# Latents stored before their norms' factors, norm sums read from transposed sums, and one mask product instead of two

## The chip, the cores and the metric

The kernel runs on one core of a Trainium2 chip. The metric is the device time of one execution in microseconds (us): the median over three runs of the kernel before is 1730.43 us (1730.31 to 1732.46). "The kernel before" is the program without the change; the profile below was taken of one of its executions.

A core has five engines that work through their own instruction streams in order and meet at semaphores: PE multiplies matrices, ACT applies functions and copies, DVE does elementwise work and reductions, POOL does small work and issues some DMAs, SP issues the other DMAs. PE writes to PSUM, which has eight banks of 128 x 512 float32 each; ACT and DVE carry results from there to SBUF.

## The reference

The program is a trunk of two layers over 512 tokens of width 1024, in float32. Each layer adds two blocks to the token stream `x`:

```
x = x + OutProj(sum over i of sigmoid(gate_i) * BranchProj_i(mixer_i(RMSNorm(x))))
x = x + ConvFFN(RMSNorm(x))
```

The three mixers are neighbourhood attention on a grid (NA), latent attention (MLA, four heads), and windowed grouped attention with sinks (GQA, eight heads). They share one input projection. What matters here:

```
def rmsnorm(x, g):   y = x * rsqrt(mean(x*x) + EPS);  return y * g
MLA: q  = rmsnorm(c_q,  g_qa)  @ w_uq      c_q: 384 wide,  a projection of rmsnorm(x)
     kv = rmsnorm(c_kv, g_kva) @ w_ukv     c_kv: 256 wide, a projection of rmsnorm(x)
     p  = softmax((q_nope k_nope + rope(q_pe) rope(k_pe)) * 192 ** -0.5);  out = p v
GQA: scores with |i - j| > 128 are masked; a sink logit joins the softmax
```

Since an RMS norm multiplies each token by one number, that number can be applied to the input or to whatever is linear in it. There are two norms in a row in front of MLA: the norm of `x` (one factor per token, called r1 below), and the norm of the latent `c_q` or `c_kv`.

## The kernel before, in words

Activations lie with features on the partitions and the 512 tokens along the free dimension. Each product in float32 is made of three products of rounded parts: `mm3` (L158) issues, for each block of 128 rows, high by high (L162), low weights or activations by high (L163) and high by low (L164), each with 512 columns. `split` (L145) makes the two parts: ACT casts the high one (L148, or L151 with a factor), DVE subtracts it (L149, L152). Weights come by DMA into `raw` (three buffers), are split into `whi` and `wlo` (three buffers each), and are fetched three entries ahead of their use. So a weight's cast waits until PE is through with the weight three entries earlier.

The order of PE's and SP's work is written out by hand in `schedule` (a list of steps, run one by one); the orders of ACT and DVE are set by a scheduler at build time, which sees priorities (`PRIO`, `ATTN_PRIO`) and its own estimates. On the chip every engine keeps the order that it was given.

The factor of a norm is made in three steps. `sumsq` adds the squares of the feature blocks (ACT squares, DVE adds), `rs_tokens` (L184) adds over the partitions with four products of `acc` by a column of ones (L188), takes the mean on DVE (L190) and the power -1/2 on POOL (L192), which leaves a tile `rt` of 128 x 4 (a factor per token, tokens on partitions). `rs_spread` (L195) turns it with four transpositions (L200) into `rb`, the factor along the free dimension, repeated on all partitions.

The front of the MLA stage runs so in each layer: the products `lat` (four latent blocks) and `lat4` (the fifth), with the norm sums and the spread of r1 in between; `latent` multiplies each block by `rb` (L155), squares it, and, for the key and value blocks, splits it. Then `rs_q` (sums of the query latent), `kr` (the rotary key, L424), `rb_q` (spread of the query factor, which multiplies the three query blocks again on DVE before they are split), `rs_k`, the values `v`, a gate, `rb_k`, then the rotary queries `qr`, the first head's `qn` and `kn`, a gate, the second head's, and the attention.

The attention steps: `ms(h, half)` makes the scores of two blocks of 128 queries (L492 to L496, five products each, in one of three banks `ps_s`), then DVE takes the negated row maximum (`nm`, L498), ACT the exponential with its row sum (`pt`, L500), DVE the reciprocal (L501) and ACT the scaling (L502). `mt(h, half)` transposes `pt` of all four blocks (L509) and splits the result into `ph`, `pl`; `mp(h, half)` multiplies by the values into `ps_po`, which `split` moves to `yah`, `yal`. PE's order there is `ms(h+1, 0)`, `mt(h, 0)`, `qn` and `kn` of head h+2, `mp(h, 0)`, `mt(h, 1)`, `ms(h+1, 1)`, `mp(h, 1)`, and then the same for the next h.

In GQA, `gs` makes the scores of one head and one query block (L761, L762), adds the masks of the left and right neighbour blocks by products with an identity in bf16 (L764, L766; both in the two inner blocks of queries, one in each outer block), and goes on as MLA does, with two score banks.

## Time and profile before

| | value |
|---|---|
| time, median of 3 runs | 1730.43 us (1730.31 to 1732.46) |
| the profiled execution | 1730.6 us |
| its span in the trace | 1728.8 us |
| PE busy | 1715.1 us, 99% |
| DVE busy | 1155.6 us, 67% |
| ACT busy | 857.9 us, 50% |
| POOL busy | 31.2 us, 2% |
| share of PE in the chain that ended last | 91% |

The span is the time from the first to the last traced instruction; 1.8 us of the execution lie around it. Matmuls overlap: the next one starts long before the end that the trace draws for the last, so the distance between two starts is what a product costs PE, not its drawn length. A time in square brackets behind an instruction is how long its engine sat idle before it, and what it waited for.

### The profile page before, as it was taken

The page shows a single profiled execution, that of the slowest core. Times are in us where ns is not written, and L with a number is a line of the kernel's source. Part 1 is how long each engine was busy: PE and PEld are TensorE (multiplying, and loading weights), DVE is VectorE, ACT ScalarE, POOL GpSimd, SP SyncE. Part 2 cuts the span into 40 slices and gives each one's busy share as a digit, 9 for nine tenths or more (in the row PEclk, how much of TensorE's full clock was granted, in tenths as well). Part 3 has the DMA queues.
Part 4 walks back from the last instruction along what each step waited for, and adds up shares of the span by engine and source line. Part 5 has one row for each costly group of instructions (what it writes and reads, how often), then busy time and mean ns, then how long its engine had stood idle before and what let it go on. Part 6 is the DMA issues. An engine that isn't in the chain of part 4 may idle for free.

```text
span 1728.8 us, 21460 instructions
## 1 busy us (share of the span) xinstructions
PE 1715.1 (99%) x8106; PEld 1427.5 (83%) x8106; DVE 1155.6 (67%) x1872; ACT 857.9 (50%) x1492; POOL 31.2 (2%) x74
## 2 busy tenths in 40 slices
PE   9999999999999999999999999999999999999998
PEld 7788888888888888888887888888788888888887
DVE  6767885877558777734357678768875587777234
ACT  6774655665335444433247656557544354444232
POOL 1000000000000000000000000000000000000000
PEclk9999999999999999999999999999999999999999
DMA  5222233222333333323232232332223333333231
GB/s 175 72 77 83 80 95 94 68 68 62 105 91 116 96 95 97 97 89 107 80 92 83 74 86 71 99 90 68 62 73 110 97 98 98 98 98 98 85 104 67
DMA packets 290695, 155.38 MB, mean 90 GB/s; under 512 B 8672, under 2 KB 287072, under 8 KB 290592
## 3 DMA queue, kind: packets, MB, share of 16 engines
q1 hardware_dynamic: 288288, 148.92, 29.9%
q0 software_dynamic: 2016, 4.72, 0.9%
q8 instruction: 63, 1.03, 0.2%
q10 hardware_dynamic: 288, 0.38, 0.1%
q14 instruction: 40, 0.33, 0.1%
HBM read 151.89 MB, written 2.10 MB: 89 GB/s over the span
## 4 chain that ended last, share of the span: by engine, by line
PE 91%; DVE 4%; ACT 2%; issue 2%; DMA 0%; SPq 0%; POOLq 0%; POOL 0%; DVEq 0%; ACTq 0%
PE ps_d L162 20%; PE ps_d L164 20%; PE ps_d L163 20%; PE ps_g L163 7%; PE ps_g L162 7%; PE ps_g L164 7%; DVE wlo L149 1%; PE ps_po L653 1%; PE ps_tp L789 1%; PE ps_tp L638 1%; PE ps_tp L509 1%; ACT rsw L211 1%; PE ps_s L761 0%; PE ps_s L620 0%; PE ps_s L619 0%
## 5 line engine op out<-in xcount | busy, mean ns | idle before, releaser
L148 ACT CAST whi<-raw 128x1024 fp32r<-128x1024 f32 (+4 forms) x340 | 302.2, 889 | 611.9 <-PE ps_d L163 330.6
L162 PE MATMUL ps_d<-hh,whi 128*128 128x512 f32 x1328 | 520.5, 392 | 0.0
L164 PE MATMUL ps_d<-hh,wlo 128*128 128x512 f32 x1328 | 517.1, 389 | 0.0
L163 PE MATMUL ps_d<-hl,whi 128*128 128x512 f32 x1328 | 516.9, 389 | 0.0
L149 DVE TENSOR_TENSOR wlo<-raw,whi 128x1024 fp32r<-128x1024 f32 (+3 forms) x338 | 345.1, 1021 | 199.6 <-ACT whi L148 199.1
L164 PEld LDWEIGHTS ps_d<-hh,wlo 128*128 128x128 f32 x1328 | 249.3, 188 | 52.3
L162 PEld LDWEIGHTS ps_d<-hh,whi 128*128 128x128 f32 x1328 | 249.5, 188 | 50.6 <-DVE rot L155 0.6
L163 PEld LDWEIGHTS ps_d<-hl,whi 128*128 128x128 f32 x1328 | 249.5, 188 | 50.3
L162 PE MATMUL ps_g<-ff,whi 128*128 128x512 f32 x334 | 129.9, 389 | 0.0
L163 PE MATMUL ps_g<-ff,whi 128*128 128x512 f32 x334 | 129.9, 389 | 0.0
L164 PE MATMUL ps_g<-ff,wlo 128*128 128x512 f32 x334 | 129.9, 389 | 0.0
L155 DVE TENSOR_TENSOR u<-ps_d,rb 128x512 f32<-128x512 f32 x80 | 55.3, 691 | 65.0 <-PE ps_d L164 65.0
L155 DVE TENSOR_TENSOR gz<-ps_d,rb 128x512 f32<-128x512 f32 x48 | 33.2, 691 | 76.5 <-PE ps_d L164 76.3
L851 ACT ACTIVATE c<-u,par 128x512 f32<-128x512 f32 x88 | 71.7, 815 | 5.1 <-DVE u L155 2.8
L149 DVE TENSOR_TENSOR pl<-ps_tp,ph 128x512 fp32r<-128x512 f32 x104 | 69.2, 682 | 6.7 <-ACT ph L148 6.6
L162 PEld LDWEIGHTS ps_g<-ff,whi 128*128 128x128 f32 x334 | 62.7, 188 | 13.1
L164 PEld LDWEIGHTS ps_g<-ff,wlo 128*128 128x128 f32 x334 | 62.7, 188 | 13.0
L163 PEld LDWEIGHTS ps_g<-ff,whi 128*128 128x128 f32 x334 | 62.7, 188 | 12.9
L853 DVE SCALAR_TENSOR_TENSOR c<-u,par,c 128x511 f32<-128x511 f32 x88 | 66.0, 750 | 2.7
L852 DVE SCALAR_TENSOR_TENSOR c<-u,par,c 128x511 f32<-128x511 f32 x88 | 65.6, 745 | 0.6 <-ACT c L851 0.6
L857 ACT ACTIVATE c<-c 128x512 f32<-128x512 f32 x44 | 27.8, 631 | 76.6 <-DVE c L853 76.6
L148 ACT CAST ph<-ps_tp 128x512 fp32r<-128x512 f32 x104 | 57.6, 587 | 5.9 <-PE ps_tp L509 2.8
(280 smaller groups left out, 2624.6 us busy)
## 6 DMA issues: line engine op xcount, KB each, us to landing
raw<-in_w_in_dram SPq DMA_DIRECT2D x86, 512.0 KB, 3.9
raw<-in_w_up_dram SPq DMA_DIRECT2D x80, 512.0 KB, 3.7
raw<-in_w_down_dram SPq DMA_DIRECT2D x32, 512.0 KB, 3.5
raw<-in_w_down_dram SPq DMA_DIRECT2D x16, 384.0 KB, 3.0
raw<-in_w_in_dram SPq DMA_DIRECT2D x18, 256.0 KB, 2.9
raw<-in_w_br_mla_dram SPq DMA_DIRECT2D x16, 256.0 KB, 2.6
raw<-in_w_br_na_dram SPq DMA_DIRECT2D x16, 256.0 KB, 2.6
raw<-in_w_br_gqa_dram SPq DMA_DIRECT2D x16, 256.0 KB, 2.6
```

The source lines that it names most:

```text
L148: nc.scalar.copy(hi, src)
L149: nc.vector.tensor_sub(lo, src, r32(hi))
L155: self.nc.vector.tensor_tensor(out, a, b, ALU.mult)
L162: mm(ps, sh, mh, start=first and k == 0, stop=False)
L163: mm(ps, sh, ml, start=False, stop=False)
L164: mm(ps, sl, mh, start=False, stop=last and k == n - 1)
L211: nc.scalar.copy(sw[32 * i:32 * i + 32, :], ps[32 * j:32 * j + 32, :])
L509: self.nc.tensor.transpose(tp[:, b * P:(b + 1) * P], self.pts[h, b][:, kc * P:(kc + 1) * P], self.idf)
L851: nc.scalar.activation(c, u, AF.Identity, bias=pr[:, PC_CB + fi:PC_CB + fi + 1], scale=cw[:, 1:2])
L852: nc.vector.scalar_tensor_tensor(c[:, 1:], u[:, :S - 1], cw[:, 0:1], c[:, 1:], ALU.mult, ALU.add)
L853: nc.vector.scalar_tensor_tensor(c[:, :S - 1], u[:, 1:], cw[:, 2:3], c[:, :S - 1], ALU.mult, ALU.add)
L857: nc.scalar.activation(c, c, AF.Gelu_apprx_tanh)
```

## The change

Four things change.

1. `latent` no longer multiplies by `rb`. The blocks are split straight from PSUM, and squared straight from PSUM. The query blocks are not multiplied by their own factor either: `rb_q` is gone with its four transpositions. The missing factors are applied later: the query's (times r1 and the softmax scale) as the scale operand of the exponential, and by one more small DVE instruction on the maximum, `nm`; the key's and value's in the split of the values and in `rb_k`, which carried the latent norm's factor already.
2. `rs_tokens` transposes the four blocks of `acc` and lets DVE add along the free dimension; the mean and epsilon move from DVE to POOL. For the two latent norms POOL also multiplies the sums by r1 squared, and the result by r1 (or by r1 times the softmax scale). POOL runs two, or four, instructions where it ran one.
3. The step `qr` moves from behind `rb_k` to between `rs_k` and the values.
4. In the two inner query blocks of GQA one mask product over both neighbour blocks takes the place of two.

The diff (empty lines left out):

```diff
--- before.py
+++ after.py
@@ -181,27 +181,32 @@
         nc.vector.tensor_add(acc, acc, sq)
         return acc
-    def rs_tokens(self, pool, acc, dim):
+    def rs_tokens(self, acc, dim, latent=None):
         nc = self.nc
         ps = self.bank("r")
         for j in range(4):
-            nc.tensor.matmul(ps[:, j:j + 1], acc[:, j * P:(j + 1) * P], self.ones, start=True, stop=True)
+            nc.tensor.transpose(ps[:, j * P:(j + 1) * P], acc[:, j * P:(j + 1) * P], self.idf)
         ms = self.small.tile([P, 4], F32, tag="ms", name="ms", bufs=2)
-        nc.vector.tensor_scalar(ms, ps[:, 0:4], 1.0 / dim, EPS, ALU.mult, ALU.add)
+        nc.vector.tensor_reduce(ms, ps[:].rearrange("p (j c) -> p j c", j=4), AX.X, ALU.add)
+        if latent:
+            nc.gpsimd.tensor_tensor(ms, ms, latent[0], ALU.mult)
+        nc.gpsimd.tensor_scalar(ms, ms, 1.0 / dim, EPS, ALU.mult, ALU.add)
         rt = self.small.tile([P, 4], F32, tag="rt", name="rt", bufs=3)
         nc.gpsimd.tensor_tensor(rt, ms, self.neghalf, ALU.pow)
+        if latent:
+            nc.gpsimd.tensor_tensor(rt, rt, latent[1], ALU.mult)
         return rt
-    def rs_spread(self, rt, rb, scale=None):
+    def rs_spread(self, rt, rb):
         ps = self.bank("r")
         for j in range(4):
             self.nc.tensor.transpose(ps[:, j * P:(j + 1) * P], rt[:, j:j + 1].to_broadcast([P, P]), self.idf)
-        if scale is None:
-            self.nc.scalar.copy(rb, ps)
-        else:
-            self.nc.scalar.activation(rb, ps, AF.Copy, scale=scale)
+        self.nc.scalar.copy(rb, ps)
     def rope(self, pool, ps, rows, ct, st, nb=2):
         nc = self.nc
@@ -272,7 +277,7 @@
                             for k0, nk in ((0, 8), (8, 8), (16, 6)) for m in range(4)]
         gate = iter([("gate", b, m) for b in (1, 0, 2) for m in range(8)]).__next__
-        s = ["mla_open", "lat", "lat4", "rs_q", "kr", "rb_q", "rs_k", ("v", 0), ("v", 1), gate(), "rb_k", "qr"]
+        s = ["mla_open", "lat", "lat4", "rs_q", "kr", "rs_k", "qr", ("v", 0), ("v", 1), gate(), "rb_k"]
         s += [("qn", 0), ("kn", 0), gate(), "mla_attn", ("qn", 1), ("kn", 1), ("ms", 0, 0), ("ms", 0, 1), gate()]
         for h in range(3):
             dn = [("qn", h + 2), ("kn", h + 2)] if h < 2 else [("naq", 0)]
@@ -349,19 +354,12 @@
         self.split(hi, lo, self.x[k], g[:, k:k + 1])
         self.h.append((hi, lo))
-    def norm_hooks(self, evac, late=False):
-        def sums():
-            self.rt = self.rs_tokens(self.const, self.acc, D)
-        def spread():
-            self.rb = self.const.tile([P, S], F32, tag="rb", name="rb")
-            self.rs_spread(self.rt, self.rb)
-            evac(0)
-            evac(1)
-        if late:
-            return {(1, 0): sums, (1, 2): lambda: (spread(), evac(2)), (1, 3): lambda: evac(3)}
-        return {(0, 3): sums, (1, 1): spread, (1, 2): lambda: evac(2), (1, 3): lambda: evac(3)}
+    def norm_sums(self):
+        self.rt = self.rs_tokens(self.acc, D)
+    def norm_spread(self):
+        self.rb = self.const.tile([P, S], F32, tag="rb", name="rb")
+        self.rs_spread(self.rt, self.rb)
     def do_mla_open(self):
@@ -389,10 +387,17 @@
         return self.mxt(f"{t}h{k}", F32R), self.mxt(f"{t}l{k}", F32R)
     def do_lat(self):
-        self.c, self.lat, self.qacc, self.kacc = [], [None] * 5, None, None
+        self.lat, self.qacc, self.kacc = [None] * 5, None, None
         self.qtags, self.ktags = ["acc", "sq1"], ["yah0", "yal0"]
-        self.group(self.W["lat"], self.h, 
-                   self.norm_hooks(lambda i: self.latent(LAT[i], self.gbank[i]), self.l == 0))
+        lat = lambda j: self.latent(LAT[j], self.gbank[j])
+        early = [(0, 3), (1, 1)] if self.l else [(1, 0), (1, 2)]
+        hooks = {(1, j): [lambda j=j: lat(j)] for j in range(4)}
+        hooks.setdefault(early[0], []).append(self.norm_sums)
+        hooks.setdefault(early[1], []).append(self.norm_spread)
+        self.group(self.W["lat"], self.h, {k: (lambda fs=fs: [f() for f in fs]) for k, fs in hooks.items()})
+        self.r1 = self.small.tile([P, 8], F32, tag="r1", name="r1")
+        self.nc.gpsimd.tensor_tensor(self.r1[:, 0:4], self.rt, self.rt, ALU.mult)
+        self.nc.gpsimd.tensor_scalar(self.r1[:, 4:8], self.rt, MLA_SCALE, None, ALU.mult)
     def do_lat4(self):
         if self.l == 0:
@@ -401,20 +406,18 @@
         self.latent(4, self.dense(self.spec(), self.h))
     def latent(self, i, ps):
+        tags = ((f"mg{i}", f"mg{i + 4}") if i < 3 else ("mg3", "mg7") if i == 3 else ("yah3", "yal3"))
+        self.lat[i] = [self.mxt(t, F32R) for t in tags]
+        self.split(*self.lat[i], ps, self.pr[:, PC_QA + i:PC_QA + i + 1])
         if i < 3:
-            c = self.mxt(("yah1", "yal1", "yah2")[i])
-            self.mul(c, ps, self.rb)
-            self.qacc = self.sumsq(self.const, c, self.qacc, self.qtags)
-            self.c.append(c)
-            return
-        c = self.mp.tile([P, S], F32, tag="ev", name="ev", bufs=2)
-        self.mul(c, ps, self.rb)
-        self.kacc = self.sumsq(self.mx, c, self.kacc, self.ktags)
-        self.lat[i] = self.mxt(("mg3", "yah3")[i - 3], F32R), self.mxt(("mg7", "yal3")[i - 3], F32R)
-        self.split(*self.lat[i], c, self.pr[:, PC_QA + i:PC_QA + i + 1])
+            self.qacc = self.sumsq(self.const, ps, self.qacc, self.qtags)
+        else:
+            self.kacc = self.sumsq(self.mx, ps, self.kacc, self.ktags)
     def do_rs_q(self):
-        self.rtq = self.rs_tokens(self.mp, self.qacc, 384.0)
+        self.rtq = self.rs_tokens(self.qacc, 384.0, [self.r1[:, 0:4], self.r1[:, 4:8]])
     def do_kr(self):
         st = self.weights(self.spec())
@@ -431,16 +434,8 @@
         self.stack(self.kr[0], t, 0)
         self.swap(self.kr[1], self.kr[0])
-    def do_rb_q(self):
-        rbq = self.mxt("yal2")
-        self.rs_spread(self.rtq, rbq, MLA_SCALE)
-        for i in range(3):
-            self.mul(self.c[i], self.c[i], rbq)
-            self.lat[i] = self.mxt(f"mg{i}", F32R), self.mxt(f"mg{i + 4}", F32R)
-            self.split(self.lat[i][0], self.lat[i][1], self.c[i], self.pr[:, PC_QA + i:PC_QA + i + 1])
     def do_rs_k(self):
-        self.rtk = self.rs_tokens(self.mp, self.kacc, 256.0)
+        self.rtk = self.rs_tokens(self.kacc, 256.0, [self.r1[:, 0:4], self.rt])
     def do_v(self, half):
         if half == 0:
@@ -496,8 +491,9 @@
             mm(s, self.qr[h][:, bs], self.kr[1], start=False, stop=True)
             nm = self.small.tile([P, 2], F32, tag="nm", name="nm", bufs=6)
             nc.vector.tensor_reduce(nm[:, 0:1], s, AX.X, ALU.max, negate=True)
+            nc.vector.tensor_scalar(nm[:, 0:1], nm[:, 0:1], self.rtq[:, b:b + 1], None, ALU.mult)
             pt = self.mp2.tile([P, S], F32, tag="pt", name="pt", bufs=6)
-            nc.scalar.activation(pt, s, AF.Exp, bias=nm[:, 0:1], accum_out=nm[:, 1:2])
+            nc.scalar.activation(pt, s, AF.Exp, bias=nm[:, 0:1], scale=self.rtq[:, b:b + 1], accum_out=nm[:, 1:2])
             nc.vector.reciprocal(nm[:, 1:2], nm[:, 1:2])
             nc.scalar.activation(pt, pt, AF.Copy, scale=nm[:, 1:2])
             self.pts[h, b] = pt
@@ -760,10 +756,9 @@
             s = self.bank("s")
             mm(s[:, :w], self.gqs[h][:, bs], self.gk[g][0][:, ks], start=True, stop=False)
             mm(s[:, :w], self.gqs[h][:, bs], self.gk[g][1][:, ks], start=False, stop=False)
-            if b > 0:
-                mm(s[:, 0:P], self.idb, self.gmask[:, 0:P], start=False, stop=b == 3)
-            if b < 3:
-                mm(s[:, w - P:w], self.idb, self.gmask[:, P:2 * P], start=False, stop=True)
+            sv = s[:, :w].rearrange("p (k c) -> p k c", c=P)[:, (nk - 1 if b == 0 else 0):(1 if b == 3 else nk):2]
+            mm(sv, self.idb, self.gmask[:].rearrange("p (k c) -> p k c", c=P)[:, b == 0:2 - (b == 3)],
+               start=False, stop=True)
             nc.vector.tensor_reduce(nm[:, hh:hh + 1], s[:, :w], AX.X, ALU.max, negate=True)
             nc.vector.tensor_scalar(nm[:, hh:hh + 1], nm[:, hh:hh + 1], HD_SCALE, self.nsink[:, h:h + 1],
                                     ALU.mult, ALU.min)
@@ -838,7 +833,9 @@
             self.fps, self.fp = self.open("ff")
             self.ff = []
             ups = [0, NF, 1, NF + 1]
-            self.group(self.W["up"], self.h, self.norm_hooks(lambda i: self.conv(ups[i], self.gbank[i])))
+            conv = lambda *js: [self.conv(ups[j], self.gbank[j]) for j in js]
+            self.group(self.W["up"], self.h, {(0, 3): self.norm_sums, (1, 1): lambda: (self.norm_spread(), conv(0, 1)),
+                                              (1, 2): lambda: conv(2), (1, 3): lambda: conv(3)})
         else:
             self.conv(fi, self.dense(self.spec(), self.h))```

The scheduler at build time makes new orders for ACT and DVE in the MLA stage of each layer, and at one place of GQA. Three places matter; both layers have the same order. Numbers in names tell buffers apart.

On ACT, at the second head of the attention. `ps_po_...` is the product `mp(0, 1)`, `pt_960`, `pt_972` (before) and `pt_957`, `pt_970` (after) are the last two query blocks of head 1, `pt_994` and `pt_993` the first of head 2. Before:

```order
L500 ACTIVATE pt_960,nm_958<-ps_s_952,nm_958 128x512
L500 ACTIVATE pt_972,nm_970<-ps_s_964,nm_970 128x512
L148 CAST yah0_982<-ps_po_927 128x512
L502 ACTIVATE pt_960<-pt_960,nm_958 128x512
L502 ACTIVATE pt_972<-pt_972,nm_970 128x512
L500 ACTIVATE pt_994,nm_992<-ps_s_986,nm_992 128x512
```

On ACT at the same place of the changed program:

```order
L148 CAST yah0_980<-ps_po_923 128x512
L496 ACTIVATE pt_957,nm_954<-ps_s_948,nm_954,rt_440 128x512
L496 ACTIVATE pt_970,nm_967<-ps_s_961,nm_967,rt_440 128x512
L498 ACTIVATE pt_957<-pt_957,nm_954 128x512
L496 ACTIVATE pt_993,nm_990<-ps_s_984,nm_990,rt_440 128x512
L498 ACTIVATE pt_970<-pt_970,nm_967 128x512
```

The cast of `ps_po` moved ahead of the two exponentials, and an exponential of the next head moved between the two scalings. The same happens one head later.

On DVE, at the same place (`yal` is the low part of `ps_po`). Before:

```order
L498 TENSOR_REDUCE nm_958<-ps_s_952 128x1
L498 TENSOR_REDUCE nm_970<-ps_s_964 128x1
L501 RECIPROCAL nm_958<-nm_958 128x1
L501 RECIPROCAL nm_970<-nm_970 128x1
L498 TENSOR_REDUCE nm_992<-ps_s_986 128x1
L149 TENSOR_TENSOR yal0_983<-ps_po_927,yah0_982 128x512
```

On DVE at the same place of the changed program:

```order
L493 TENSOR_REDUCE nm_954<-ps_s_948 128x1
L493 TENSOR_REDUCE nm_967<-ps_s_961 128x1
L494 TENSOR_SCALAR nm_954<-nm_954,rt_440 128x1
L494 TENSOR_SCALAR nm_967<-nm_967,rt_440 128x1
L149 TENSOR_TENSOR yal0_981<-ps_po_923,yah0_980 128x512
L493 TENSOR_REDUCE nm_990<-ps_s_984 128x1
L497 RECIPROCAL nm_954<-nm_954 128x1
L494 TENSOR_SCALAR nm_990<-nm_990,rt_440 128x1
L497 RECIPROCAL nm_967<-nm_967 128x1
```

The two reciprocals now stand behind the low part of `ps_po` and behind the next head's maximum.

On ACT, in the front of the MLA stage, between the values and the second gate (`whi` 128x1024 is that gate's weight). Before:

```order
L225 CAST kr<-kr 64x512
L224 CAST kr<-kr 64x512
L211 COPY rsw<-ps_d 32x512 x4
L148 CAST whi<-raw 128x1024
L211 COPY rsw<-ps_d 32x512 x4
```

On ACT in the changed program, from the copies of the rotary key (`ev`) towards that weight:

```order
L216 COPY rsw<-ev 32x512 x2
L216 COPY rsw<-ps_d 32x512 x4
L148 CAST whi<-raw 128x384
L151 ACTIVATE ynh_564<-ps_d,rt 128x512
L225 CAST kr<-rot 64x512
L216 COPY rsw<-ps_d 32x512 x4
L151 ACTIVATE ynh_575<-ps_d,rt 128x512
L151 ACTIVATE ynh_586<-ps_d,rt 128x512
L230 CAST kr<-kr 64x512
L148 CAST whi<-raw 128x256
L151 ACTIVATE ynh_597<-ps_d,rt 128x512
L225 CAST qr<-rot 64x512 x2
```

Behind the last of these rows come one more `kr` cast, two more `qr` casts, and then the gate's weight: all of the rotary queries' work on ACT now precedes it.

## Rows read from the trace of the kernel before

**Rows 1.** The page, part 1: busy us (share of span) and instructions.
```profile
PE 1715.1 (99%) x8106; PEld 1427.5 (83%) x8106; DVE 1155.6 (67%) x1872; ACT 857.9 (50%) x1492; POOL 31.2 (2%) x74
```

**Rows 2.** Waits of PE: us in total, times, longest.
```profile
PE ps_s L492 <- ACT pt L500: 2.7, 2, 1.3
...
PE ps_po L163 <- DVE pl L149: 0.5, 2, 0.2
```

**Rows 3.** Timeline of PE around norm sums and spread: start us, us, instruction.
```profile
21.00 0.94 PE L188 MATMUL ps_r<-cst,acc 128*128 128x1 f32 x8
...
22.13 0.40 PE L163 MATMUL ps_g<-hl,whi 128*128 128x512 f32 x1
...
27.16 0.39 PE L164 MATMUL ps_g<-hh,wlo 128*128 128x512 f32 x1
27.39 0.60 PE L200 MATMUL ps_r<-idf,rt 128*128 128x128 f32 x4
...
28.06 0.39 PE L163 MATMUL ps_g<-hl,whi 128*128 128x512 f32 x1
```

**Rows 4.** Timeline of PE, scores and masks of an inner GQA block.
```profile
375.26 0.34 PE L762 MATMUL ps_s<-gk,gq 128*128 128x384 f32 x1
375.44 0.23 PE L764 MATMUL ps_s<-gmask,idb 128*128 128x128 bf16 x1
...
375.54 0.42 PE L761 MATMUL ps_s<-gk,gq 128*128 128x384 f32 x1
375.79 0.34 PE L762 MATMUL ps_s<-gk,gq 128*128 128x384 f32 x1
```

**Rows 5.** Timeline, all engines, first attention scores of layer 0.
```profile
72.98 1.28 DVE L498 TENSOR_REDUCE nm<-ps_s 128x1 f32<-128x512 f32 x2
...
73.70 0.69 ACT L500 ACTIVATE pt<-ps_s,nm 128x512 f32<-128x512 f32 x1 [0.91 <-DVE nm L498]
...
74.53 0.50 PE L492 MATMUL ps_s<-kn,qn 128*128 128x512 f32 x1 [1.33 <-ACT pt L500]
```

**Rows 6.** ACT's groups by form, 40 to 70 us: busy us, mean ns.
```profile
L211 ACT COPY rsw<-ps_d 32x512 f32<-32x512 f32 x8 | 4.6, 579 | 0.1
L151 ACT ACTIVATE ynh<-ps_d,rt 128x512 fp32r<-128x512 f32 x4 | 2.7, 686 | 1.0 <-POOL rt L192 0.9
L220 ACT CAST qr<-rot 64x512 fp32r<-64x512 f32 x4 | 2.5, 620 | 1.1 <-DVE rot L215 1.0
L148 ACT CAST whi<-raw 128x1024 fp32r<-128x1024 f32 x2 | 2.1, 1053 | 0.0
```

**Rows 7.** Timelines of DVE and PE at the second gate of layer 0.
```profile
59.75 1.22 DVE L149 TENSOR_TENSOR wlo<-raw,whi 128x1024 fp32r<-128x1024 f32 x1
...
61.24 0.39 PE L164 MATMUL ps_d<-hh,wlo 128*128 128x512 f32 x1
```

**Rows 8.** Timelines of ACT, DVE, PE at `mt(1, 0)` of layer 0.
```profile
92.84 0.69 ACT L500 ACTIVATE pt<-ps_s,nm 128x512 f32<-128x512 f32 x1 [1.97 <-DVE nm L498]
...
94.18 0.58 ACT L148 CAST yah<-ps_po 128x512 fp32r<-128x512 f32 x1
94.65 1.35 ACT L502 ACTIVATE pt<-pt,nm 128x512 f32<-128x512 f32 x2
...
95.00 0.69 DVE L498 TENSOR_REDUCE nm<-ps_s 128x1 f32<-128x512 f32 x1 [0.52 <-PE ps_s L496]
...
96.81 0.15 DVE L501 RECIPROCAL nm<-nm 128x1 f32<-128x1 f32 x1
...
95.94 1.04 PE L509 MATMUL ps_tp<-idf,pt 128*128 128x128 f32 x8
```

**Rows 9.** Timelines of POOL and DVE in the front of layer 0's MLA stage.
```profile
37.24 1.93 POOL L192 TENSOR_TENSOR rt<-ms,cst 128x4 f32<-128x4 f32 x1 [13.74 <-DVE ms L190]
42.77 1.01 POOL L192 TENSOR_TENSOR rt<-ms,cst 128x4 f32<-128x4 f32 x1 [3.59 <-DVE ms L190]
...
37.08 1.23 DVE L149 TENSOR_TENSOR wlo<-raw,whi 128x1024 fp32r<-128x1024 f32 x1
```

## The prediction

> **What bounds the kernel now.** I read the busy times first: PE works for 99% of the span, DVE for 67%, ACT for half of it, POOL for next to nothing [rows 1]. So an instruction taken from PE is worth its whole price, one taken from DVE or ACT is worth something only where PE waits for it. Then I read PE's waits [rows 2]: the longest is 1.3 us, once per layer, for the first scores of MLA, and all waits together are few. What the list does not show are stalls that hide under the drawn ends of products; distances between starts show them. A 512-column product costs 0.23 us of PE (27.16 to 27.39) [rows 3] though it is drawn 0.39 long; I use 0.227, the mean of long stretches. The reader is to see that PE has almost no slack and that almost every stall is in MLA's attention or in GQA: any wait that a new order of ACT and DVE makes there goes straight into the time.
>
> **What PE loses in work.** The sum is made against the profiled execution, 1730.6 us (span 1728.8 and 1.8 around it), which is 0.2 above the median of 1730.43.
>
> Norm sums: the eight passes over the ones column and the product behind them take from 21.00 to the next product's start at 22.13, 1.13 us; less one product, 0.90 [rows 3]. Four transpositions, measured likewise at the spread, take 28.06 - 27.39 - 0.227 = 0.44. There are four norm sums per layer (two norms of `x`, two of latents), eight in all: 8 x 0.46 = 3.7 us saved. The new ones move 128 columns just as those of the spread do, so I take that price as it is.
>
> The query factor's spread goes: 2 x 0.44 = 0.9 us.
>
> Masks: 32 inner pairs (2 layers, 2 key heads, 2 inner blocks, 4 heads). From the second score product to the next scores' second product it is 375.79 - 375.26 = 0.53 us with a pair between; two 384-column products alone cost about 2 x 0.17 (0.18 to the mask) [rows 4]. So a pair costs 0.19. A single product of 256 columns saves at most the second's share, some 0.07, and at least nothing, since the same columns pass. By columns (128 more cost about 0.055, the step from 384 to 512 columns) I take 0.02: 32 x 0.02 = 0.7 us, with bounds 0 and 2.3.
>
> Work in all: 5.3 us less. The one added chain, DVE's reduction over 512 columns in place of 4 (0.69 against some 0.15) and one to three more POOL instructions, lies beside two weights' products (over 5 us) between each norm sum and its spread. That cover is large: the norms of `x` stay hidden.
>
> **What PE loses or gains in waits, per layer.** I follow ACT and DVE in their new orders, with durations from the rows, in layer 0's times; layer 1 has the same order.
>
> First scores. PE waits 1.33 us by the trace because DVE comes to the first maxima only at 72.98, with a backlog, and the bank is free only after the exponential of 73.70 [rows 5]; counted by starts the stall is 1.5. Now DVE has eight multiplications of 0.67 less in front and two longer reductions more, so the backlog is gone. From the scores' start at s: the first are ready at s + 1.3, the maximum takes 0.69, the low part of `kn`, which stands between, 0.6, the new scaling 0.1, the exponential 0.69, the release some 0.1, that is s + 3.5 to 3.7; PE wants the bank at s + 3.4. Stall 0.1 to 0.3 instead of 1.5: a gain of 1.2, with bounds 0 and 1.5.
>
> Second gate. PE asks for the low part of its weight at 61.24 and it is ready at 59.75 + 1.22 = 60.97 [rows 7]; a slack of 0.27. With three sums and a spread saved PE asks at 61.24 - 3 x 0.46 - 0.44 = 59.4. On ACT all copies and casts of the rotary queries now stand in front of this weight's cast. PE's rotary key ends 83 products and two turns earlier, at 39.8; then the first gate's cast (1.05), its low part (1.22), DVE's longer reduction (0.69) and two steps of the key (1.3) must pass before ACT may copy: 44.1. From there ACT does ten copies (0.58 to 0.62), four value parts (0.69), four query casts (0.62), three key casts of the same length and two small weights (0.9 together) [rows 6]: 13.8 drawn, about 13.4 start to start, then the cast of 1.05 and DVE's 1.22. That gives 59.9: PE waits 0.6 us. Bounds 0 (ACT a little quicker) and 2.
>
> Head 2's first transpositions, `mt(1, 0)`. Before, ACT takes the exponentials at 92.84, the cast of `ps_po` at 94.18, both scalings from 94.65 to 96.0, and PE transposes from 95.94, the last block some 0.3 later: just in time [rows 8]. In the new order ACT sits at the cast of `ps_po` until its product has ended, about 93.9. Then it runs the cast (0.5), two exponentials (0.7 each, to 95.7), and waits for the reciprocal, which DVE has behind the low part and head 2's maximum (95.0 to 95.7 even before): 95.9. Scaling (0.6), head 2's exponential (0.7), second scaling (0.7): 97.9. PE needs it at 96.3. Wait 1.6, with the restart 1.75. Bounds 0.5 and 2.2. No other work is in PE's queue: it is in order, and the transpositions hold up `qn` and `kn` of head 3, which do not need them.
>
> Behind it PE comes 1.75 later to `mp(1, 1)`, where it loses 0.9 now waiting for low parts (the list shows 0.5 of it in both layers together [rows 2], the rest is under drawn ends). DVE's queue there hangs on `kn` of head 3, so it moves along; I get 0.5, a gain of 0.4.
>
> The next head, `mt(2, 0)`: the same order, the same count from the end of `ps_po`: 1.5, bounds 0.5 and 2.2. Head 3 has a gate of 5.4 us between; no wait.
>
> GQA: at one place per layer a 1.05 us weight cast [rows 6] now stands ahead of an exponential whose bank PE waits for; two banks, about 0.3, bounds 0 and 1.
>
> Per layer: -1.2 + 0.6 + 1.75 - 0.4 + 1.5 + 0.3 = +2.55; twice: 5.1 us.
>
> **Sum.** 1730.6 - 5.3 + 5.1 = 1730.4 us. What the change takes from PE, its new order in the attention gives back.
>
> **POOL.** The latent factors now pass through four POOL instructions. One power took 1.01 us, and one 1.93, when it was issued beside a DVE subtraction with both inputs in SBUF (37.08 to 38.31) [rows 9]. The trace has no POOL multiplication of this shape; the power is the nearest row and bounds it from above, nothing from below. DVE's reduction ends at about 42.8 and ACT needs the value factor at 48.1: 5.3 us for four instructions. At 1.01 each they take 4.0: hidden. The query factor is wanted 25 us later.
>
> The Trainium skill (SBUF — State Buffer, section Who interferes with whom) says that a DVE instruction with two SBUF inputs contends with a GpSimd instruction that reads SBUF, and that the later one blocks until the other is done. The 1.93 us row agrees, since it ends about one power after the subtraction's end; by that rule each of the four can be held up by the rotary key's multiplications, which is the second rival below.
>
> **The rivals.**
>
> Faster: the two new waits before the transpositions do not come, since the cast of `ps_po` and the products meet otherwise than I count. For it: the wait rests on sums of ten steps, and both blocks were in time before. Against it: the order is fixed and each step has a row. Then only 1.2 is gained at the first scores, 0.6 lost at the gate, 0.3 in GQA: -5.3 + 2 x (-1.2 + 0.6 + 0.3) = -5.9, so 1724.7; with half of the waits, 1727.5.
>
> Slower: the value factor comes late. At 1.93 for each POOL instruction it is ready at 42.8 + 7.7 = 50.5, 2.4 us after ACT needs it, and ACT's chain to the second gate hangs on it: PE waits 0.6 + 2.4 there. That is 2 x 2.4 more, 1735.2. It decides from a chain of 5.3 us on. For it: the row of 1.93 is of this very stage. Against it: during the chain DVE has only two such instructions and then idles.
>
> Not what it says: transpositions of `acc` or the strided mask cost more than their kin, so that less than 5.3 is saved; without any of the mask and half of the sums, 1733.
>
> **How the numbers follow.** A difference under 0.2% (3.5 us) cannot be told from none for this kernel. Forecast (1727 to 1734, its own range): 0.47. Faster rival: 0.28. Slower rival: 0.17; less saved: 0.08, half of it beyond 3.5 us when waits are longer as well. So faster 0.28, same 0.47 + 0.04 = 0.51, slower 0.17 + 0.04 = 0.21. The range reaches from 1725.3, close to the faster rival, to 1734.6, short of the slower one.
>
> **What would show it.** In the profile after: the norm sums as four transpositions with the next product 0.6 us behind; PE's wait at the first scores down from 1.3 to at most 0.3; in the list of PE's waits a new entry, transpositions waiting for ACT's scaled `pt`, twice per layer, 1 to 2 us each; a wait of about half a us at the second gate for `wlo`; POOL's four instructions ended 5 us after DVE's reduction. The forecast is wrong if PE's transpositions wait under 0.5 us, or if the second gate waits over 2.

## The result, and the profile after

The changed kernel takes 1732.93 us (median of 20 runs, 1732.27 to 1735.04), the kernel before 1730.70 us in the 20 runs beside them. The ratio is 1.0014 with a 95% interval of 1.0008 to 1.0020: 2.2 us slower, small but real. The forecast was 1730.4 us, no change; the time lies above it, inside the range. The profiled execution took 1732.3 us (span 1730.5).

Part 1 of the page, in the form of [rows 1]:

```profile
PE 1711.9 (99%) x8034; PEld 1420.3 (82%) x8034; DVE 1156.5 (67%) x1888; ACT 858.2 (50%) x1490; POOL 38.4 (2%) x94
```

PE is busy 3.2 us less and the program is longer all the same: time went into waits. PE's waits in the changed kernel (us in total, times, longest), to be read against [rows 2]:

```profile
PE ps_tp L505 <- ACT pt L498: 4.0, 4, 1.0
PE ps_d L164 <- DVE wlo L149: 1.7, 2, 0.9
PE ps_s L487 <- ACT pt L496: 1.2, 4, 0.3
PE ps_tp L784 <- DVE pt L775: 1.2, 4, 0.3
...
PE ps_r L191 <- DVE acc L181: 0.7, 2, 0.4
```

All five are new, new in kind or longer. The first is the wait before `mt(1, 0)` and `mt(2, 0)` that was forecast; the second is the second gate, also forecast, but at about half its size; the fourth stands before transpositions in GQA and was 0.5 us in two places before; the fifth, transpositions that wait for the sum of the key latent's squares, was not forecast. The 2.7 us of [rows 2] at the first scores are gone: what is left there is part of the third.

The norm sum and the spread, PE's timeline (start us, us), against [rows 3]:

```profile
20.63 0.60 PE L191 MATMUL ps_r<-idf,acc 128*128 128x128 f32 x4
20.99 0.47 PE L162 MATMUL ps_g<-hh,whi 128*128 128x512 f32 x1
21.30 0.39 PE L163 MATMUL ps_g<-hl,whi 128*128 128x512 f32 x1
```

From 20.63 to the second product at 21.30 it is 0.67 us, that is 0.44 for four transpositions beside one product of 0.227, as counted.

The first scores of layer 0, timelines of DVE, ACT and PE, against [rows 5]:

```profile
70.48 0.69 DVE L493 TENSOR_REDUCE nm<-ps_s 128x1 f32<-128x512 f32 x1
...
71.93 0.78 ACT L496 ACTIVATE pt<-ps_s,nm,rt 128x512 f32<-128x512 f32 x1 [1.15 <-DVE nm L494]
...
72.85 0.50 PE L487 MATMUL ps_s<-kn,qn 128*128 128x512 f32 x1
```

The first maximum is taken at 70.48 instead of 72.98, so the bank is free in time but for 0.3 us by starts.

`mt(1, 0)` of layer 0, timelines of ACT, DVE and PE, against [rows 8]:

```profile
92.25 0.59 ACT L148 CAST yah<-ps_po 128x512 fp32r<-128x512 f32 x1 [3.03 <-PE ps_po L164]
92.73 0.78 ACT L496 ACTIVATE pt<-ps_s,nm,rt 128x512 f32<-128x512 f32 x1
...
94.26 0.72 ACT L498 ACTIVATE pt<-pt,nm 128x512 f32<-128x512 f32 x1
94.89 0.76 ACT L496 ACTIVATE pt<-ps_s,nm,rt 128x512 f32<-128x512 f32 x1
...
95.64 0.71 ACT L498 ACTIVATE pt<-pt,nm 128x512 f32<-128x512 f32 x1
...
91.67 0.33 DVE L494 TENSOR_SCALAR nm<-nm,rt 128x1 f32<-128x1 f32 x2
...
93.66 0.50 PE L487 MATMUL ps_s<-kn,qn 128*128 128x512 f32 x1 [0.32 <-ACT pt L496]
...
96.41 0.77 PE L505 MATMUL ps_tp<-idf,pt 128*128 128x128 f32 x5 [0.99 <-ACT pt L498]
```

ACT is idle for 3.03 us, the scaled maxima are there at 92.0, and the exponentials wait behind a cast whose product ends at 92.2. They come 0.7 late, so PE misses a score bank at 93.66, and the second scaling, behind an exponential of the next head, lets PE go on only at 96.41. The wait at the bank, 0.6 us by starts (see the experiments), was not forecast. It adds nothing to the sum: PE goes on when the second scaling has ended, and what it lost at the bank it waits less there.

The second gate of layer 0, timelines of ACT, DVE and PE, against [rows 7]:

```profile
57.53 1.05 ACT L148 CAST whi<-raw 128x1024 fp32r<-128x1024 f32 x1
...
57.90 1.41 DVE L226 TENSOR_TENSOR qr<-rot,qr 64x512 fp32r<-64x512 f32 x2
59.34 1.69 DVE L149 TENSOR_TENSOR wlo<-raw,whi 128x1024 fp32r<-128x1024 f32 x2
...
60.62 0.50 PE L164 MATMUL ps_d<-hh,wlo 128*128 128x512 f32 x1 [0.92 <-DVE wlo L149]
```

ACT casts the weight at 57.53, near to where my sum puts it (59.9 less 1.22 and 1.05 is about 57.6; this run is 0.3 ahead from its first 16 us, so the sum was right to 0.3). But DVE then has two subtractions of the rotary queries in front, and the low part starts 0.76 after the cast has ended.

The front of the MLA stage in layer 0, ACT, DVE and PE at the key latent's sum:

```profile
36.11 0.68 ACT L151 ACTIVATE yah<-ps_d,par 128x512 fp32r<-128x512 f32 x1
38.34 0.60 ACT L180 ACTIVATE sq<-ps_d 128x512 f32<-128x512 f32 x1 [1.55 <-DVE yal L152]
...
35.82 0.69 DVE L193 TENSOR_REDUCE ms<-ps_r 128x4 f32<-128x512 f32 x1 [3.12 <-PE ps_r L191]
36.43 1.21 DVE L149 TENSOR_TENSOR wlo<-raw,whi 128x1024 fp32r<-128x1024 f32 x1
37.56 0.74 DVE L152 SCALAR_TENSOR_TENSOR yal<-ps_d,par,yah 128x512 fp32r<-128x512 f32 x1
38.97 0.69 DVE L181 TENSOR_TENSOR acc<-acc,sq 128x512 f32<-128x512 f32 x1 [0.66 <-ACT sq L180]
...
39.05 0.39 PE L427 MATMUL ps_d<-hl,whi 128*128 128x512 f32 x1
39.72 0.66 PE L191 MATMUL ps_r<-idf,acc 128*128 128x128 f32 x4 [0.28 <-DVE acc L181]
```

ACT's square reads the same bank `ps_d` as DVE's low part `yal`, and stands behind it: here the readers of one bank on two engines follow one another. Of ACT's 1.55 us of waiting, 0.74 are this low part; before it DVE was busy with the low part of a weight, from 36.43 to 37.64. So the sum is made at 39.66, PE wanted it at 39.28. This agrees with the Trainium skill (PSUM — Partial Sum Buffer, section PSUM bank collisions raise a hardware error): two engines may not access one bank and quadrant at once, reads included, so software orders them.

### The profile page after: what moved, and what is told of

The parts are those of the page before. It is cut to its first block, busy times and chain, and to the rows that moved or that the text cites. A ratio compares the mean times of both kernels' runs of the same rounds, so it can differ in the third digit from the quotient of the medians.

```text
span 1730.5 us, 21339 instructions
## 1 busy us (share of the span) xinstructions
PE 1711.9 (99%) x8034; PEld 1420.3 (82%) x8034; DVE 1156.5 (67%) x1888; ACT 858.2 (50%) x1490; POOL 38.4 (2%) x94
## 3 DMA queue, kind: packets, MB, share of 16 engines
q8 instruction: 63, 1.03, 0.3%
## 4 chain that ended last, share of the span: by engine, by line
PE 93%; ACT 3%; DVE 3%; issue 1%; POOLq 0%; POOL 0%; DVEq 0%; ACTq 0%
PE ps_d L162 21%; PE ps_d L164 21%; PE ps_d L163 21%; PE ps_g L163 7%; PE ps_g L164 7%; PE ps_g L162 7%; PE ps_tp L784 1%; PE ps_po L649 1%; PE ps_tp L634 1%; ACT pt L496 1%; PE ps_s L757 1%; PE ps_tp L505 1%; DVE wlo L149 1%; PE ps_s L758 0%; ACT rsw L216 0%
## 5 line engine op out<-in xcount | busy, mean ns | idle before, releaser
L148 ACT CAST whi<-raw 128x1024 fp32r<-128x1024 f32 (+4 forms) x340 | 302.2, 889 | 606.7 <-PE ps_d L163 339.5
L162 PE MATMUL ps_d<-hh,whi 128*128 128x512 f32 x1328 | 520.5, 392 | 0.0
L164 PE MATMUL ps_d<-hh,wlo 128*128 128x512 f32 x1328 | 517.3, 390 | 1.7 <-DVE wlo L149 1.7
L163 PE MATMUL ps_d<-hl,whi 128*128 128x512 f32 x1328 | 517.0, 389 | 0.0
L149 DVE TENSOR_TENSOR wlo<-raw,whi 128x1024 fp32r<-128x1024 f32 (+3 forms) x338 | 344.9, 1021 | 189.9 <-ACT whi L148 189.5
L164 PEld LDWEIGHTS ps_d<-hh,wlo 128*128 128x128 f32 x1328 | 249.3, 188 | 54.7 <-DVE wlo L149 2.6
L162 PEld LDWEIGHTS ps_d<-hh,whi 128*128 128x128 f32 x1328 | 249.6, 188 | 50.8 <-DVE rot L155 0.5
L163 PEld LDWEIGHTS ps_d<-hl,whi 128*128 128x128 f32 x1328 | 249.5, 188 | 50.2
L162 PE MATMUL ps_g<-ff,whi 128*128 128x512 f32 x334 | 129.9, 389 | 0.0
L163 PE MATMUL ps_g<-ff,whi 128*128 128x512 f32 x334 | 129.9, 389 | 0.0
L164 PE MATMUL ps_g<-ff,wlo 128*128 128x512 f32 x334 | 129.9, 389 | 0.0
L155 DVE TENSOR_TENSOR u<-ps_d,rb 128x512 f32<-128x512 f32 x80 | 55.3, 691 | 65.1 <-PE ps_d L164 65.1
L155 DVE TENSOR_TENSOR gz<-ps_d,rb 128x512 f32<-128x512 f32 x48 | 33.2, 691 | 78.3 <-PE ps_d L164 78.0
L162 PEld LDWEIGHTS ps_g<-ff,whi 128*128 128x128 f32 x334 | 62.7, 188 | 13.1
L164 PEld LDWEIGHTS ps_g<-ff,wlo 128*128 128x128 f32 x334 | 62.7, 188 | 13.0
L163 PEld LDWEIGHTS ps_g<-ff,whi 128*128 128x128 f32 x334 | 62.7, 188 | 13.0
L149 DVE TENSOR_TENSOR pl<-ps_tp,ph 128x512 fp32r<-128x512 f32 x104 | 68.6, 682 | 6.0 <-ACT ph L148 5.9
L148 ACT CAST ph<-ps_tp 128x512 fp32r<-128x512 f32 x104 | 57.0, 585 | 7.3 <-PE ps_tp L505 3.9
```

The costliest lines, as they stand in the source:

```text
L148: nc.scalar.copy(hi, src)
L149: nc.vector.tensor_sub(lo, src, r32(hi))
L155: self.nc.vector.tensor_tensor(out, a, b, ALU.mult)
L162: mm(ps, sh, mh, start=first and k == 0, stop=False)
L163: mm(ps, sh, ml, start=False, stop=False)
L164: mm(ps, sl, mh, start=False, stop=last and k == n - 1)
```

## The experiments

Times are medians, each beside the kernel before on the same chip; intervals are 95%. They are about 0.1% (1.6 us) to either side, so smaller effects are read from two traces: the start of the same product in both, and the places where the distance of the two jumps. "By starts" means this; the first 16 us, which differ from run to run, are left out of it.

**The square ahead of the split** (the changed kernel with)

```diff
     def latent(self, i, ps):
-        self.split(*self.lat[i], ps, self.pr[:, PC_QA + i:PC_QA + i + 1])
         if i < 3:
             self.qacc = self.sumsq(self.const, ps, self.qacc, self.qtags)
         else:
             self.kacc = self.sumsq(self.mx, ps, self.kacc, self.ktags)
+        self.split(*self.lat[i], ps, self.pr[:, PC_QA + i:PC_QA + i + 1])
```

> The changed kernel with the square of each latent block ahead of its split. Theory (the second latent sum comes late because ACT's square stands behind DVE's low part of the same bank): PE's wait of its transpositions for the sum (0.7 us in two entries, 0.44 and 0.60 by starts) goes, about 1.0 us in all, 1731.9 us. Rival (the sum is late because DVE is busy with a 1.2 us weight part at that time, whatever the square does): the wait stays at 0.7 and the time at 1732.9.

1731.24 us beside 1730.29: 0.9 above before instead of 2.2 (ratio 1.0006, 0.9997 to 1.0015). By starts 0.44 and 0.60 less, at these two transpositions and nowhere else. In its trace, ACT, DVE and PE:

```profile
36.15 0.59 ACT L180 ACTIVATE sq<-ps_d 128x512 f32<-128x512 f32 x1
...
36.48 1.21 DVE L149 TENSOR_TENSOR wlo<-raw,whi 128x1024 fp32r<-128x1024 f32 x1
37.61 0.68 DVE L181 TENSOR_TENSOR acc<-acc,sq 128x512 f32<-128x512 f32 x1
38.21 0.74 DVE L152 SCALAR_TENSOR_TENSOR yal<-ps_d,par,yah 128x512 fp32r<-128x512 f32 x1
...
39.32 0.60 PE L191 MATMUL ps_r<-idf,acc 128*128 128x128 f32 x4
```

The weight part on DVE is as long as ever and the wait is gone: the theory holds.

**The cast behind the exponentials** (the changed kernel with an order on ACT alone: `issue_after` queues what is traced in it behind an instruction, without a wait)

```diff
-            nc.scalar.activation(pt, s, AF.Exp, ...)
+            self.ex = nc.scalar.activation(pt, s, AF.Exp, ...)
...
-            self.split(*self.y[1, h], self.po)
+            with self.tc.issue_after(self.ex.ins):
+                self.split(*self.y[1, h], self.po)
```

> The changed kernel with ACT's cast of the attention product kept behind the two exponentials, as in the kernel before. Theory (the transpositions of heads 1 and 2 wait because of this cast's place): the four waits of transpositions for the scaled pt (4.0 us in the list, 2 x 1.75 per layer by starts with the bank waits that go with them) go: 6 to 7 us less, 1726 to 1727. Rival (the waits come from the longer chain of maximum, scaling of the maximum, exponential with a scale, reciprocal, and only change place): at most half of it goes, 1729.5 or more.

1729.23 beside 1730.29 (0.9995, 0.9986 to 1.0004), by starts 3.1 less than the changed kernel: half, as the rival had it. The bank wait at 93.66 goes, the transpositions still wait 0.5 us and more. ACT and PE:

```profile
92.73 0.77 ACT L496 ACTIVATE pt<-ps_s,nm,rt 128x512 f32<-128x512 f32 x1
...
93.49 0.58 ACT L148 CAST yah<-ps_po 128x512 fp32r<-128x512 f32 x1
93.95 1.34 ACT L498 ACTIVATE pt<-pt,nm 128x512 f32<-128x512 f32 x2
...
95.35 0.77 PE L505 MATMUL ps_tp<-idf,pt 128*128 128x128 f32 x5 [0.28 <-ACT pt L498]
```

In the order of before the chain is still longer than it was: two scalings of maxima (0.33) and twice 0.09 of exponential make 0.5, and before there was no slack.

**The norm sums alone** (the kernel before with)

```diff
-            nc.tensor.matmul(ps[:, j:j + 1], acc[:, j * P:(j + 1) * P], self.ones, start=True, stop=True)
+            nc.tensor.transpose(ps[:, j * P:(j + 1) * P], acc[:, j * P:(j + 1) * P], self.idf)
...
-        nc.vector.tensor_scalar(ms, ps[:, 0:4], 1.0 / dim, EPS, ALU.mult, ALU.add)
+        nc.vector.tensor_reduce(ms, ps[:].rearrange("p (j c) -> p j c", j=4), AX.X, ALU.add)
+        nc.gpsimd.tensor_scalar(ms, ms, 1.0 / dim, EPS, ALU.mult, ALU.add)
```

> The kernel before with the norm sums by transposition alone (reduction on DVE, mean on POOL). Theory (8 x 0.46 us of PE's work, with the longer chain hidden): 1730.7 - 3.7 = 1727.0. Rival (the longer chain or the new order of ACT and DVE that it brings makes PE wait): 1729 to 1731.

1727.15 beside 1730.29: 3.1 us faster (0.9982, 0.9973 to 0.9991). By starts each of the eight sums gives 0.45 to 0.49, and 0.3 per layer is lost again at the second gate's `wlo`, to which PE now comes sooner. No sum waits.

**The mask alone** (the kernel before with the mask lines of the change, in short)

```diff
-            if b > 0:
-                mm(s[:, 0:P], self.idb, self.gmask[:, 0:P], ...)
-            if b < 3:
-                mm(s[:, w - P:w], self.idb, self.gmask[:, P:2 * P], ...)
+            mm(sv, self.idb, self.gmask[:].rearrange("p (k c) -> p k c", c=P)[:, b == 0:2 - (b == 3)], ...)
```

> The kernel before with one mask product in place of two in the 32 inner pairs, alone. Theory (a pass costs by its columns, and the same columns pass): 0.02 each, 0.7 us less, 1730.0. Rival (each product has a price of its own of 0.07): 2.3 less, 1728.4. Second rival (the new order of ACT in the GQA stage brings waits): 1730.7 or more.

1729.28 beside 1730.29 (0.9994, 0.9985 to 1.0003); by starts 1.05 less. The interval does not tell theory and rivals apart, but the starts do. PE's products in the changed kernel, where the mask product is the same, against [rows 4]:

```profile
376.60 0.33 PE L758 MATMUL ps_s<-gk,gq 128*128 128x384 f32 x1
376.77 0.28 PE L760 MATMUL ps_s<-gmask,idb 128*128 128x256 bf16 x1
376.81 0.42 PE L757 MATMUL ps_s<-gk,gq 128*128 128x384 f32 x1
```

From the second score product to the next product it is 0.21 us (376.60 to 376.81) where it was 0.28 (375.26 to 375.54); the medians over the pairs are 0.216 in this run and 0.275 in the kernel before. So one product in place of two saves 0.06 a pair, 1.9 us in 32 pairs: three times the theory, near to the first rival's price. The second rival came too, in part: in each layer PE loses about 0.2 at a score bank, where ACT now casts a weight ahead of an exponential, and 0.23 at a transposition, whose cause was not followed. Together that takes 0.8 of the 1.9 back.

**The gate's weight first** (the changed kernel; `self.cast` is ACT's last weight cast, here that of the second gate)

```diff
-                self.stack(q, t, j)
+                self.stack(q, t, j) if i == 0 else self.late.append((q, t, j))
...
-        ps = self.dense(self.spec(), self.lat[:3])
+        ps = self.dense(self.spec(), self.lat[:3]); self.late_rotary()
...
+    def late_rotary(self):
+        with self.tc.issue_after(self.cast.ins):
+            while self.late: self.stack(*self.late.pop(0))
```

> The changed kernel with the second half of the rotary queries' casts (ACT) and subtractions (DVE) kept behind the second gate's weight cast; nothing else moves. The base is the changed kernel at 2.1 us above the kernel before, on this chip some 1732.4. Theory (these four steps hold up that weight's low part): PE's wait for wlo (1.7 us in two entries, 1.2 per layer by starts) goes, 2.3 us less, 1730.1. Rival (the work only moves behind the gate and DVE comes late to the first scores' maxima): their wait rises by as much, the time stays near 1732.

1730.53 beside 1730.95 (0.9997, 0.9989 to 1.0006). By starts 1.17 and 1.08 less at the two gates, and no more wait for the first scores than in the changed kernel. DVE, with no wait on PE behind it:

```profile
58.81 1.22 DVE L149 TENSOR_TENSOR wlo<-raw,whi 128x1024 fp32r<-128x1024 f32 x1
60.06 1.40 DVE L226 TENSOR_TENSOR qr<-rot,qr 64x512 fp32r<-64x512 f32 x2
...
60.56 0.39 PE L164 MATMUL ps_d<-hh,wlo 128*128 128x512 f32 x1
```

The four steps of the rotary queries, two on ACT and two on DVE, for which nobody waits yet, were together the whole of this wait. The run moves all four, so it does not tell ACT's share from DVE's.

**The cast behind the scalings** (the changed kernel, with `issue_after` as above, but behind the scaling of L498)

```diff
-            nc.scalar.activation(pt, pt, AF.Copy, scale=nm[:, 1:2])
+            self.ex = nc.scalar.activation(pt, pt, AF.Copy, scale=nm[:, 1:2])
```

> The changed kernel with ACT's cast of the attention product kept behind the two scalings, not only behind the two exponentials. Moving it behind the exponentials gave 3.1 us by the trace and left transpositions waiting 0.65 us at each of four places. Theory (what is left is the cast's 0.5 us between exponential and scaling, against the longer chain of scaled maximum and exponential): the four waits fall under 0.2 us, 2 us less than with the cast behind the exponentials, 1727.1. Rival (the longer exponentials and the scaling of the maximum set the end by themselves): no gain over 1729.2.

1728.91 beside 1730.95 (0.9988, 0.9979 to 0.9997), by starts 4.1 less than the changed kernel: 1.0 more than behind the exponentials, not 2. The transpositions' wait nearly goes, and another comes:

```profile
PE ps_po L163 <- DVE pl L149: 2.0, 2, 1.0
...
PE ps_tp L505 <- ACT pt L498: 0.2, 1, 0.2
```

With ACT's new order the scheduler put a maximum on DVE ahead of the low parts for `mp(1, 1)` (a maximum at 103.99, low parts from 104.59), and PE, sooner by what it gained, waits there. The theory was right on the wait that it named and wrong on the sum.

**The latents alone** (the changed kernel with the two mask products and)

```diff
-            nc.tensor.transpose(ps[:, j * P:(j + 1) * P], acc[:, j * P:(j + 1) * P], self.idf)
+            nc.tensor.matmul(ps[:, j:j + 1], acc[:, j * P:(j + 1) * P], self.ones, start=True, stop=True)
...
-        nc.vector.tensor_reduce(ms, ps[:].rearrange("p (j c) -> p j c", j=4), AX.X, ALU.add)
+        nc.vector.tensor_copy(ms, ps[:, 0:4])
```

> The changed kernel with the norm sums by the ones column again (DVE copies the four sums, POOL takes the mean) and the two mask products again: the kernel before plus the latents' part alone. Theory (the parts add up: 2.1 of the whole, 3.1 of the sums, 1.0 of the masks): 6.2 us slower than before, 1736.5. Rival (the waits come from the parts' company, since shorter sums bring PE earlier to the gate): the latents alone cost at most 3, 1733.

1735.93 beside 1730.95: 5.0 slower (1.0027, 1.0017 to 1.0037), so this part alone is the loss; 1.2 less than the whole and the other two parts let expect. Here the key latent's sum has no wait, and PE waits 0.43 and 0.34 less at the two second gates.

**All three** (the changed kernel with the diffs of the square ahead of the split, the gate's weight first and the cast behind the scalings)

> The changed kernel with three edits: squares ahead of the split, the second half of the rotary queries behind the gate's weight cast, the attention product's cast behind both scalings. Theory (the three waits are apart and their gains add: 1.0, 2.3 and 5.3): 1732.4 - 8.6 = 1723.8. Rival (the waits share a cause in DVE's load and partly come back at the next place): 1727 or more.

1725.04 beside 1730.95: 5.9 us faster than before (0.9963, 0.9951 to 0.9976) and so about 8 faster than the changed kernel; by starts 7.7, which is 1.0, 2.3 and 4.1 and a little. The gains add; the expectation had the third one too large.

**Low parts first, on top of the three**

```diff
+            with self.tc.issue_after((self.pl if half else self.rec[h - 1, 2]).ins) if h > 1 else ExitStack():
                 nc.vector.tensor_reduce(nm[:, 0:1], s, AX.X, ALU.max, negate=True)
```

(`pl` is the last low part, `rec` the reciprocal of the head before)

> The version with all three edits, which ran at 1725.0, and the maxima of the second halves of heads 2 and 3 kept on DVE behind the low parts of the transposed weights of the head before (and the next head's first maximum behind the reciprocal, its place there). Theory (with the cast behind both scalings the low parts came one maximum of 0.68 later than with the cast behind the exponentials, and PE waited 1.0 us for them once per layer): that wait falls by one maximum, 0.65 per layer, 1.3 us less, 1723.7. Rival (the wait is set by the gate weight's low part of 1.2 us further ahead on DVE, or the later maxima make the next transpositions late): no gain, 1725.

1725.18 beside 1730.89 (0.9970, 0.9959 to 0.9981): nothing gained. By starts 0.60 is won at `mp(1, 1)`, as expected, 0.5 lost at once at the next bank and 0.1 at the next transpositions: the later maxima make the exponentials late. The rival was right.

**Sums and mask without the latents** (the kernel before with the diffs of the norm sums alone and the mask alone)

> The kernel before with the norm sums by transposition and the single mask product, without the latents' part. Theory (the two parts do not touch each other): 1730.9 - 3.1 - 1.0 = 1726.8, which is 1.8 slower than the version with the latents' part and its three edits. Rival (the shorter sums take the cover from something in the GQA stage or at the second gate): 1728 or more.

1727.02 beside 1730.89 (0.9979, 0.9970 to 0.9987): the two add up. Against it the version with the latents and three edits has another 2 us by the medians, though the intervals overlap, and by starts it saves 5.8 us where this one saves 4.0.

**The scale operand** (the kernel before with)

```diff
-            nc.scalar.activation(pt, s, AF.Exp, bias=nm[:, 0:1], accum_out=nm[:, 1:2])
+            nc.scalar.activation(pt, s, AF.Exp, bias=nm[:, 0:1], scale=self.ones, accum_out=nm[:, 1:2])
```

> The kernel before with a scale operand on the exponentials of the latent attention: a column of ones per partition in place of none, so that nothing else changes. In the changed kernel this exponential is drawn 0.78 us long, before 0.69. Theory (the operand is what costs): 0.78 here too, 32 x 0.09 = 2.9 us more of ACT, of which PE feels only what stands in its chains, two exponentials at the transpositions of heads 1 and 2, at most 0.2 at each of four places: 0 to 0.8 us more, 1730.9 to 1731.7. Rival (the length comes from the larger spread of unscaled scores, not from the operand): 0.69 and no change.

1731.10 beside 1730.77 (1.0002, 0.9993 to 1.0012). The exponential's line with min, median and max ns:

```profile
L500 ACT ACTIVATE pt<-ps_s,nm,cst x32: 759/777/806, 74.0 to 977.8; 128x512 f32<-128x512 f32 x32
```

Before, the median is 689; in the changed kernel, where the operand holds factors and not ones, it is 778. So the operand costs 0.09 us, and the larger scores cost nothing. By starts PE loses 0.2 us per layer, half of it at the first scores and half at `mt(2, 0)`.

## Why the prediction was wrong, step by step

Per layer, in us, by starts:

| step | forecast | measured |
|---|---|---|
| four norm sums | -1.84 | -1.8 |
| query spread | -0.44 | -0.45 |
| first scores | -1.2 | -1.17 |
| second gate | +0.6 | +1.15 |
| `mt(1, 0)` with its bank | +1.75 | +1.83 |
| `mp(1, 1)` | -0.4 | -0.38 |
| `mt(2, 0)` with its bank | +1.5 | +1.8 |
| masks | -0.35 | -0.9 |
| waits in GQA | +0.3 | +0.5 |
| key latent's sum | 0 | +0.52 |
| together | -0.1 | +1.1 |

Twice 1.0 (the rows are rounded), less 0.3 that the changed kernel's run gained in the first 16 us, are the 1.7 us between the two spans.

The step that failed is the one that cost the norm-sum chains at nothing: "That cover is large". It speaks of the way from a sum to its spread. What comes before the sum was not followed: squares and low parts that now read one bank in turn, a reduction of 0.69 on DVE in front, and a PE that is 0.46 sooner there because of the sum before and another 0.44 because the query spread, which stood right in front, is gone. Neither part makes this wait alone (none in the latents alone, none in the sums alone); together they cost 0.44 and 0.60, and the square first takes all of it away. How much of it the reduction adds, and how much PE's coming sooner, no run separates. This wait, about 1.0, with 0.2 more at the gate, is also why the parts alone (+5.0, -3.1, -1.0) add up to +0.9 and the whole is +2.2.

The second term is one of size: the gate, 0.6 forecast and 1.15 measured. ACT's sum was right to 0.3 us; DVE's queue behind it was left out. The words "then the cast of 1.05 and DVE's 1.22" took DVE as free, though the subtractions of the queries that ACT had just cast stood there. By the trace they are 0.76 of the wait; the rest, some 0.4, is ACT's chain, which the forecast had at 0.6.

The third is the masks, mis-sized the other way: 0.02 a pair forecast, 0.06 measured. The 0.19 that the prediction read for a pair holds some 0.09 that stays: the score product behind a mask takes 0.26, with one mask product as with two, where behind a product with the values it takes 0.17. That the time came out so near to the forecast is in part luck: with the masks at the forecast's price the change would have been over 3 us slower.

What was right: the norm sums and the spread, the first scores, and that the transpositions wait for ACT's scaled `pt`, because of the order that the prediction followed; the order of ACT and DVE and durations from rows were enough to count these waits to 0.3 us. The entry in PE's waits came as forecast, 4 times 1.0. Neither of the prediction's two signs of being wrong showed (transpositions that wait under 0.5, a gate over 2), since both look at waits that it had counted. And a difference of 2.2 us could be told from none, where the prediction put the limit at 3.5.

The rival Faster fell with these waits. Slower: its mechanism came, but far too small. POOL's two chains and a multiplication on DVE, to be read against [rows 9]:

```profile
36.67 1.03 POOL L195 TENSOR_TENSOR ms<-ms,r 128x4 f32<-128x4 f32 x1 [12.33 <-DVE ms L193]
...
42.46 0.20 POOL L195 TENSOR_TENSOR ms<-ms,r 128x4 f32<-128x4 f32 x1 [2.74 <-DVE ms L193]
...
43.02 1.53 POOL L198 TENSOR_TENSOR rt<-ms,cst 128x4 f32<-128x4 f32 x1
44.63 0.20 POOL L200 TENSOR_TENSOR rt<-rt 128x4 f32<-128x4 f32 x1
...
43.00 0.68 DVE L155 TENSOR_TENSOR ev<-ev,rb 64x512 f32<-64x512 f32 x1
```

A multiplication takes 0.20, not the 1.01 of a power, and the value factor is there 2.4 us after the reduction. The rule that the prediction drew from the Trainium skill shows in the first row: issued beside DVE's `wlo` (36.43 to 37.64, two inputs in SBUF) it ends at 37.70, just behind it. The power of the second chain, issued at 43.02 beside the rotary key's multiplication (43.00 to 43.68, two inputs in SBUF), takes 1.53 instead of 1.01. Both cost nothing here, since nobody waits. "Not what it says" fell too: sums and mask alone save their 4.

## What to carry to other kernels

Work taken from the engine that bounds brings it sooner to every later meeting with the others: take each meeting's slack again with all savings in front of it, and follow the chain before a hand-over as far as the one behind it. When a copy in SBUF goes and two engines read the bank instead, their reads came one after another here, so put first the one that somebody waits for. Where a scheduler's estimates set the order, three small edits of order were worth 8 us here, almost four times what the change itself moved.

## What the hardware showed that was not expected

The profiled runs, whose programs begin alike, reach the same product between 14.9 and 17.7 us. In the profiled run of the version with all three edits (1727.0 us, its median is 1725.0) PE waits longer for its first parts, and then the products go at half speed for a while. PE's timeline, and the stretch from 8.0 to 12.5 us (us, busy us and instructions of PE, PEld, DVE, ACT and POOL, then the granted clock):

```profile
7.91 0.50 PE L162 MATMUL ps_g<-hh,whi 128*128 128x512 f32 x1 [1.30 <-ACT hh L151]
...
9.16 0.63 PE L164 MATMUL ps_g<-hh,wlo 128*128 128x512 f32 x1
9.59 0.63 PE L162 MATMUL ps_g<-hh,whi 128*128 128x512 f32 x1
...
8.00:12.50 4.50, 4.21 (x11) 3.09 (x12) 4.39 (x7) 4.35 (x8) 0.00 (x0) 0.62 1.04 338
```

The same stretch of the next version (1725.0 us), where PE's longest wait there is shorter:

```profile
8.00:12.50 4.50, 4.50 (x20) 3.33 (x20) 4.33 (x7) 4.31 (x8) 0.00 (x0) 1.00 1.10 352
```

Products 0.43 us apart (9.16 to 9.59) instead of 0.23 are PE at 1.2 of its 2.4 GHz; by starts against the changed kernel's trace this costs another 1.5 us behind the wait.

The scale operand's 0.09 us was not in my count, though the Trainium skill (ScalarE: Activation LUTs, section What ACT_TABLE_LOAD costs) states that each operand read from a column per partition adds about 93 ns. The run agrees: 777 ns against 689.
